# Search rounds spread over all tensor work, a new selection, sliding attention turned by DMA, and a gate projection moved

## The chip, the core and the metric

The kernel runs on one core of a Trainium2 chip. The metric is device time in microseconds for one execution. The profile follows five engines of the core: PE (TensorE, with its weight loads as PEld), DVE (VectorE), ACT (ScalarE), POOL (GpSimd) and SP (SyncE, which here only issues DMAs). Each takes its instructions in the order in which they were written for it.

## The reference

Two layers act on a sequence of 1024 tokens with 1024 channels. Each is an RMS norm, one input projection, two attentions whose outputs are multiplied by a gate `silu(z)`, and an output projection with a residual.

```
# layer 1
y = rms_norm(x) @ ab_w_in                    # qa ka va qi ki wi za qb kb vb zb
score = sum_h wi_h * relu(qi_h . ki)         # causal, per query
idx = top_k(score, 256)
oa = softmax(qa . ka over idx) @ va          # sparse attention, 8 heads, 2 key heads
ob = softmax with sinks over a window of 128 # sliding attention, 8 heads
x = x + concat(oa*silu(za), ob*silu(zb)) @ ab_w_out
# layer 2
oc = g0*compressed + g1*selected + g2*window attention
q  = rms_norm(cq,  d_q_lat_norm)  @ d_w_uq   # latent attention
kv = rms_norm(ckv, d_kv_lat_norm) @ d_w_ukv
od = causal softmax attention
x = x + concat(oc*silu(zc), od*silu(zd)) @ cd_w_out
```

The top-k of a query tile with 384 to 1024 causal keys (tiles 2 to 7; tiles 0 and 1 keep all keys) is needed exactly, ties resolved to the lower key index.

## The kernel before, in words

Everything is tiled by 128 tokens (8 tiles). A projection is cut into chunks of about 256 columns. For each chunk and each token tile, `fill_gen` issues 24 matmuls: the operands are split into a high and a low part, and three products (L498, L499, L500) are summed over 8 row blocks. The weights come by DMA from SP into `wraw` (L450), ACT makes the high part `whi` (L454), POOL the low part `wlo` (L455). The list `FAO` sets the order of the chunks of layer 1: `ki qi kb qb0 z0 z1 z2 qb1 ka qa0 qa1`. The `z` chunks are gates.

`attn_gen` walks a list of attention jobs. A job is one query tile and one key head, so four heads. The passes of q.k (L644, PE) go into `psS`; a DVE instruction (L647) adds the mask and leaves the scores and the negative row maximum `nm`; ACT takes the exponential with `nm` as bias (L652) into `pt`. Then up to four blocks of 128x128 at a time go through `tstage` and `cstage`: PE turns the blocks of `pt` (L672) into PSUM, they are split into two halves of 16 bits, `ph` and `pl`, scaled by `PSCALE` = 4096, and PE multiplies them with the values (L690, L691, L692). `WAYS` says how the split is made. Way `p`: ACT writes `ph` (L676) and DVE `pl` (L677). Way `q`: ACT copies to `sg` (L681), POOL writes `ph` (L682) and `pl` (L683). The sliding attention (`job_b`, 16 jobs) uses way `q` alone.

The top-k is a search for a threshold, bit by bit, on 32-bit keys that are kept as two 16-bit halves, `hi16` and `lo16`. `topk` runs 16 rounds on one half and 16 on the other. A round counts, for each tile, the keys under a candidate: tiles 2, 3 and 7 on DVE (L855), 4, 5 and 6 on ACT (L851), then two small DVE instructions move the candidate (L866, L868). After the 32nd round the selection turns the threshold into an additive mask, tile by tile: five passes over the keys on DVE (L900, L901, L903, L904, L906), one running sum (L905), and two POOL passes (L907, L908). A sparse attention job (`job_a`) of tile 2 or more waits for the mask of its tile.

`Lanes.run` interleaves the generators when the program is written: a main one (attention jobs), a filling one (projections, `ratio`), and the search (`aux`, `arate`). Each step of a generator gives its cost in nanoseconds of tensor work; a search round counts as 2000. In `run` at most one step of the search is taken for each step of the others, as long as its sum is under `TA` = 1.2 times their sum. When a job has to wait for a projection, `pump` issues projections until it is there; there the search gets no step. What is left of the search is issued after the last sliding job, by `while not searched`. Then a scheduler of the framework reorders the instructions of each engine. So the order has to be read from the built program.

Layer 2 has the same structure. Its latents `cq` and `ckv` are normed in `lat_chain` with a broadcast row of gains `glat` (L1353).

## Time and profile before

| | |
|---|---|
| three runs | 1542.68, 1544.64, 1548.07 us; median 1544.64 |
| profiled execution | 1548.08 us; its span 1546.3 us |
| mean granted clock of TensorE | 0.949 of full |
| PE busy | 1375.8 us (89%) |
| DVE busy | 1140.0 us (74%) |
| ACT busy | 898.8 us (58%) |
| POOL busy | 883.4 us (57%) |
| DMA | 93.18 MB, mean 60 GB/s |

The profile belongs to one execution, whose own time is 1548.08 us, 3.4 us above the median of the three. Busy time is the union of an engine's instructions; the rest of the span it waited. The share over the whole span mixes stretches that are bound by different engines, so the rows further below are cut by stretch.

### The profile page before, as it was taken

To read this page: it belongs to the slowest core of one execution; us is meant where nothing else is said; L and a number is where in the kernel's file an instruction comes from. 1 tells how busy PE (TensorE), PEld (TensorE's weight loads), DVE (VectorE), ACT (ScalarE), POOL (GpSimd) and SP (SyncE) were. 2 spreads that over 40 slices of the span, in tenths; PEclk is the share of its full clock that TensorE was granted. 3 is DMA by queue.
4 is the path that set the end of the run, shared out by engine and by line. 5 is a ranking of instruction groups with operands and counts; after the bars stand their busy time and mean duration, and the time that the engine had idled before them with its cause. 6 is when DMAs were issued, how large, how long until landed. Compare 5 with 4: busy or idle time off the path is not lost.

```text
span 1546.3 us, 35007 instructions
## 1 busy us (share of the span) xinstructions
PE 1375.8 (89%) x12588; PEld 1269.9 (82%) x12588; DVE 1140.0 (74%) x3431; ACT 898.8 (58%) x2451; POOL 883.4 (57%) x1194
## 2 busy tenths in 40 slices
PE   5998899865568989999999999999998678789998
PEld 5997799765467778999999998899987557678887
DVE  5387898889967856157257678976699989987763
ACT  5355698686337855145435567857666676655541
POOL 6798664885989576226255443575456566642240
PEclk9999999887779999999999999999999879989999
DMA  6311223010112233132211210011101120111232
GB/s 203 88 30 34 59 80 88 20 49 6 52 38 69 74 108 123 49 139 77 62 29 49 60 42 8 26 53 49 36 5 46 59 65 8 31 53 63 93 114 75
DMA packets 88431, 93.18 MB, mean 60 GB/s; under 512 B 20930, under 2 KB 73154, under 8 KB 88258
## 3 DMA queue, kind: packets, MB, share of 16 engines
q1 hardware_dynamic: 88256, 90.95, 19.7%
q8 instruction: 99, 1.62, 0.4%
q14 instruction: 76, 0.61, 0.1%
HBM read 67.85 MB, written 23.07 MB: 59 GB/s over the span
## 4 chain that ended last, share of the span: by engine, by line
PE 55%; DVE 23%; ACT 7%; issue 5%; DMA 5%; POOL 4%; SPq 1%; DVEq 0%; ACTq 0%; POOLq 0%
PE pp L498 8%; PE pp L500 8%; PE psS L644 8%; PE pp L499 8%; PE psT L672 6%; DVE pt L647 4%; ACT junka L851 3%; DMA wraw<-in_ab_w_in 2%; PE pp L1695 2%; PE pp L1697 2%; PE pp L1696 2%; PE po L692 2%; PE po L690 2%; PE po L691 2%; DVE pl L677 1%
## 5 line engine op out<-in xcount | busy, mean ns | idle before, releaser
L498 PE MATMUL pp<-whi,Rh 128*128 128x256 f32 (+4 forms) x1648 | 484.9, 295 | 27.9 <-ACT sq L432 10.8
L499 PE MATMUL pp<-wlo,Rh 128*128 128x256 f32 (+4 forms) x1648 | 477.0, 290 | 1.1 <-POOL wlo L455 1.1
L500 PE MATMUL pp<-whi,Rl 128*128 128x256 f32 (+4 forms) x1648 | 477.4, 290 | 0.0
L498 PEld LDWEIGHTS pp<-whi,Rh 128*128 128x128 f32 x1648 | 318.0, 193 | 34.2 <-ACT sq L432 12.3
L652 ACT ACTIVATE pt<-pt,nm 128x256 f32<-128x256 f32 (+8 forms) x384 | 246.3, 642 | 162.6 <-DVE nm L647 158.6
L499 PEld LDWEIGHTS pp<-wlo,Rh 128*128 128x128 f32 x1648 | 317.8, 193 | 3.1 <-POOL wlo L455 1.6
L500 PEld LDWEIGHTS pp<-whi,Rl 128*128 128x128 f32 x1648 | 317.4, 193 | 1.2
L455 POOL TENSOR_TENSOR wlo<-wraw,whi 128x256 fp32r<-128x256 f32 (+4 forms) x208 | 166.1, 805 | 140.4 <-ACT whi L454 129.4
L672 PE MATMUL psT<-identf,pt 128*128 128x128 f32 x1256 | 219.0, 288 | 13.0 <-DVE pl L677 5.1
L682 POOL TENSOR_SCALAR ph<-sg 128x512 f16<-128x512 f32 (+3 forms) x157 | 90.2, 577 | 141.7 <-ACT sg L681 124.2
L683 POOL TENSOR_TENSOR pl<-sg,ph 128x512 f16<-128x512 f32 (+3 forms) x157 | 165.9, 1060 | 8.3
L672 PEld LDWEIGHTS psT<-identf,pt 128*128 128x128 f32 x1256 | 150.1, 146 | 24.8 <-ACT pt L652 3.8
L454 ACT ACTIVATE whi<-wraw 128x256 fp32r<-128x256 f32 (+4 forms) x208 | 83.8, 415 | 119.6 <-DMA wraw<-in_ab_w_in 38.1
L677 DVE SCALAR_TENSOR_TENSOR pl<-psT,ph 128x512 f16<-128x512 f32 (+3 forms) x233 | 128.0, 558 | 23.9 <-ACT ph L676 23.2
L676 ACT ACTIVATE ph<-psT 128x512 f16<-128x512 f32 (+3 forms) x233 | 111.6, 492 | 51.9 <-PE psT L672 46.1
L690 PEld LDWEIGHTS <-ph 128*128 128x128 f16 x1256 | 116.8, 100 | 22.1 <-issue 7.1
L692 PEld LDWEIGHTS <-pl 128*128 128x128 f16 x1256 | 114.9, 100 | 20.9 <-POOL pl L683 6.8
L647 DVE CUSTOM_DVE_ANT_0 pt<-psS,mk 128x512 f32<-128x512 f32 (+4 forms) x208 | 107.7, 520 | 32.6 <-PE psS L644 29.7
L691 PEld LDWEIGHTS <-ph 128*128 128x128 f16 x1256 | 116.8, 100 | 12.0 <-issue 10.7
L681 ACT ACTIVATE sg<-psT 128x512 f32<-128x512 f32 (+3 forms) x157 | 83.1, 535 | 41.1 <-PE psT L672 34.0
L652 ACT ACTIVATION_READ_ACCUMULATOR pt<-pt,nm 128x1 f32 x384 | 73.1, 190 | 0.0
L1054 POOL TENSOR_TENSOR mo<-mo,nz 128x256 f32<-128x256 f32 (+1 forms) x32 | 32.2, 1009 | 68.9 <-DMA nz<-zdr 29.5
(311 smaller groups left out, 3583.4 us busy)
## 6 DMA issues: line engine op xcount, KB each, us to landing
wraw<-in_cd_w_in SPq DMA_DIRECT2D x72, 128.0 KB, 2.1
wraw<-in_ab_w_in SPq DMA_DIRECT2D x56, 128.0 KB, 2.1
xs<-in_x SPq DMA_DIRECT2D x8, 512.0 KB, 6.1
od<-mx SPq DMA_DIRECT2D x32, 128.0 KB, 1.8
wraw<-in_ab_w_out SPq DMA_DIRECT2D x32, 128.0 KB, 2.2
x<-in_x SPq DMA_DIRECT2D x8, 512.0 KB, 5.2
mo<-od SPq DMA_DIRECT2D x16, 256.0 KB, 2.7
nz<-zdr SPq DMA_DIRECT2D x16, 256.0 KB, 3.1
```

Source lines behind the costliest of these rows:

```text
L455: G.tensor_tensor(lo[:, :o], raw[:, :o], hi[:, :o].bitcast(F32), OP.subtract)
L498: T.matmul(ps, xh, hi[:, :n], start=q == 0 and k == 0, stop=False)
L499: T.matmul(ps, xh, lo[:, :n], start=False, stop=False)
L500: T.matmul(ps, xl, hi[:, :n], start=False, stop=q == 3 and k == 1)
L647: V.tensor_tensor_reduce(pt[:, j * nk + c:j * nk + c + w], ps[:, at:at + w], mask(c, w), -1.0, first, op0=OP.add, op1=OP.min, accum_out=low)
L652: S.activation(pt[:, j * nk:(j + 1) * nk], pt[:, j * nk:(j + 1) * nk], AF.Exp, scale=-1.0, bias=nm[:, h:h + 1], accum_out=sm[:, h:h + 1])
L672: T.transpose(pT[:, a], pt[:, o:o + P], identf)
L677: V.scalar_tensor_tensor(pl[:, :n], pT[:, :n], PSCALE, ph[:, :n], op0=OP.mult, op1=OP.subtract)
L683: G.tensor_tensor(pl[:, :n], sg[:, :n], ph[:, :n], OP.subtract)
L690: T.matmul(dst, ph[:, a], vh(kt, h), start=kt == 0, stop=False)
L691: T.matmul(dst, ph[:, a], vl(kt, h), start=False, stop=False)
L692: T.matmul(dst, pl[:, a], vh(kt, h), start=False, stop=kt == nt - 1)
```

## The change

It has six parts. (1) `Lanes.beside` takes steps of the search after every step of tensor work, in `pump` too, and as many as are due; the rate `TA` is 0.5 in place of 1.2. (2) After the 32nd round one more round of counts is made, which gives the number of ties to drop, and the selection then takes two ACT passes, four DVE instructions and one POOL pass for each tile. (3) The factor 4096 moves from the split into the exponential: ACT adds ln 4096 to `nm` once for each group of heads. (4) The sliding attention takes way `g`: right after the exponential ACT writes the high half of `pt` and POOL the low half side by side into `hl`, and a DMA from SP turns all of it into `ht`, so PE turns no block. The other ways write their halves into `ht` as well, and `sg` shares the buffers of `hl` (4 in place of 2). (5) The chunk `z2` stands behind `qa0`. (6) The gains of the latent norms are multiplied into the rows of `d_w_uq` and `d_w_ukv` in `small_w`, and the last stage's `xr` shares the buffers of `wraw2`.

```diff
-TA = 1.2
+TA = 0.5
-FAO = 'ki qi kb qb0 z0 z1 z2 qb1 ka qa0 qa1'
+FAO = 'ki qi kb qb0 z0 z1 qb1 ka qa0 z2 qa1'
-WAYS = ('q', 'q', 'ppq', 'pq', 'ppq', 'pq', 'ppq', 'p')
+WAYS = ('g', 'g', 'ppq', 'pq', 'ppq', 'pq', 'ppq', 'p')
...
+    def beside(self, c):
+        self.due += self.rate * (c or 0.0)
+        while self.aux is not None and self.spent < self.due:
+            try:
+                self.spent += next(self.aux)
+            except StopIteration:
+                self.aux = None
...
     def pump(self, fill, until=None):
...
             self.tick()
+            self.beside(c)
...
     def run(self, main, fill, ratio, aux=None, arate=0.0):
...
             m += y
             self.tick()
+            self.beside(y)
             while fill_on and f < ratio * m:
...
                 f += c
                 self.tick()
-                if aux_on and a < arate * (m + f):
-                    try:
-                        a += next(aux)
...
+                self.beside(c)
...
+                S.activation(nm[:, h0:h0 + per], nm[:, h0:h0 + per], AF.Copy, bias=LNP)
                 for j, h in enumerate(hs):
                     S.activation(pt[:, j * nk:(j + 1) * nk], pt[:, j * nk:(j + 1) * nk], AF.Exp, scale=-1.0,
...
+                    if way[-1] in "dg":
+                        o, w = c * P, n * P
+                        hl = wk.tile([P, 1024], F16, name="hl", bufs=HLB)[:, :2 * w]
+                        S.activation(hl[:, :w], pt[:, o:o + w], AF.Copy)
+                        (V if way[-1] == "d" else G).tensor_tensor(hl[:, w:], pt[:, o:o + w], hl[:, :w], OP.subtract)
+                        ht = wk.tile([P, 8, P], F16, name="ht", bufs=HTB)
+                        nc.sync.dma_start(ht[:, :2 * n], hl.rearrange("p (k n) -> p k n", n=P), transpose=True)
...
+        counts(lo16)
+        V.tensor_tensor(inc, cnt, tgt, OP.subtract)
+        for i in GA:
+            V.tensor_scalar(inc[:, i - 2:i - 1], inc[:, i - 2:i - 1], 0.5, None, op0=OP.mult)
+        yield 2000
         searched.append(1)
...
-            V.tensor_scalar(j, blk(hi16, i), K1[:, c], None, op0=OP.is_gt)
-            V.scalar_tensor_tensor(gt, blk(lo16, i), K0[:, c], j, op0=OP.is_gt, op1=OP.add, accum_out=cnt[:, c])
-            V.tensor_scalar(inc[:, c], cnt[:, c], -1.0, float(TOPK), op0=OP.mult, op1=OP.add)
-            V.tensor_scalar(j, blk(lo16, i), K0[:, c], None, op0=OP.is_equal)
-            V.scalar_tensor_tensor(eq, blk(hi16, i), K1[:, c], j, op0=OP.is_equal, op1=OP.mult)
+            S.activation(v, blk(hi16, i), AF.Identity, scale=-1.0, bias=K1[:, c])
+            S.activation(below, blk(lo16, i), AF.Identity, scale=-1.0, bias=K0[:, c])
+            V.scalar_tensor_tensor(v, v, 2.0 ** 18, below, op0=OP.mult, op1=OP.add)
+            V.tensor_scalar(eq, v, 0.0, None, op0=OP.is_equal)
             V.tensor_tensor_scan(pre, eq, eq, 0.0, op0=OP.add, op1=OP.max)
-            V.scalar_tensor_tensor(eq, pre, inc[:, c], eq, op0=OP.is_le, op1=OP.mult)
-            G.tensor_tensor(gt, gt, eq, OP.add)
-            G.tensor_scalar(blk(hi16, i).bitcast(BF16), gt, BIG, -BIG, op0=OP.mult, op1=OP.add)
+            V.scalar_tensor_tensor(v, pre, inc[:, c], v, op0=OP.is_gt, op1=OP.add)
+            G.tensor_scalar(blk(hi16, i).bitcast(BF16), v, 0.0, -BIG, op0=OP.is_gt, op1=OP.mult)
...
-        V.scalar_tensor_tensor(z, z, r[0], g, op0=OP.mult, op1=OP.mult)
+        V.tensor_scalar(z, z, r[0], None, op0=OP.mult)
...
+            S.activation(raw, raw, AF.Copy, scale=B["glat"][:, g + r:g + r + 1])
```

Three places of the built order show what is moved. The first is DVE at the selection. Before, the selection of the tile of 896 keys (L900 to L906, with `sel` and `junk`) stands between passes of the sliding attention (L647 with `mB`) and its small sums:

```order
L900 TENSOR_SCALAR junk_1452<-hi16_789,K1_1454 128x896
L726 TENSOR_SCALAR sm_4728<-sm_4728 128x4
L901 SCALAR_TENSOR_TENSOR sel_4766,cnt_1457<-lo16_791,K0_1455,junk_1452 128x896
L647 ISA pt_4836,nm_4834<-psS_4837,mB_98,sinkn_99 128x256
L647 ISA nm_4834 128x1
L728 RECIPROCAL rs_4813<-sm_4728 128x4
L647 ISA pt_4836,nm_4834<-psS_4844,mB_98,sinkn_99 128x256
```

Now the selections follow each other on DVE with nothing between them until the tile of 896 keys, right behind the added counts (L874) and the number of ties (L914, L916); only there the first pass of the sparse attention (tile 0) stands:

```order
L874 TENSOR_SCALAR junk,cnt<-lo_791,cand 128x1024
L914 TENSOR_TENSOR inc<-cnt,tgt 128x6
L916 TENSOR_SCALAR inc<-inc 128x1 x3
L929 SCALAR_TENSOR_TENSOR sel<-sel,junk 128x384
L930 TENSOR_SCALAR sel<-sel 128x384
L931 SCALAR_TENSOR_TENSOR junk<-sel 128x384
L932 SCALAR_TENSOR_TENSOR sel<-junk,inc,sel 128x384
L929 SCALAR_TENSOR_TENSOR sel<-sel,junk 128x512
L930 TENSOR_SCALAR sel<-sel 128x512
L931 SCALAR_TENSOR_TENSOR junk<-sel 128x512
L932 SCALAR_TENSOR_TENSOR sel<-junk,inc,sel 128x512
```

All sliding jobs stand ahead of round 18 now. From round 28 on, and through the selections up to the tile of 768 keys, PE has no instruction at all. Before, 20 of the 64 passes of the sliding attention stood behind round 32, and projections with them.

The second place is SP, in the second half of the sliding attention. Before, it issues weight loads (`wraw`), and stores of results (`od<-mx`):

```order
L450 DMA wraw_5195<-in_ab_w_in 128x256
L450 DMA wraw_5258<-in_ab_w_in 128x256
L755 DMA od_101<-mx_4313 128x256
L450 DMA wraw_5264<-in_ab_w_in 128x256
L450 DMA wraw_5382<-in_ab_w_in 128x256
L755 DMA od_101<-mx_4441 128x256
L450 DMA wraw_5388<-in_ab_w_in 128x256
```

Now the transposing DMAs, which wait for POOL's `hl`, stand in the same queue ahead of weight loads:

```order
L680 DMA_TRANSPOSE ht_2574<-hl_2571 128x8x128
L680 DMA_TRANSPOSE ht_2579<-hl_2576 128x8x128
L455 DMA wraw_3585<-in_ab_w_in 128x256
L455 DMA wraw_3591<-in_ab_w_in 128x256
L680 DMA_TRANSPOSE ht_2670<-hl_2667 128x8x128
L680 DMA_TRANSPOSE ht_2675<-hl_2672 128x8x128
L774 DMA od_101<-mx_2773 128x256
L455 DMA wraw_3918<-in_ab_w_in 128x256
```

There are 30 of them in the program. Counted over all engines in the order of the build, 4 to 39 matmuls, 21 in the median, stand on PE between the issue of one and the first matmul that reads it (L709, which was L690).

The third place is ACT, in a sliding job of the first half. Before, the exponentials (L652) follow DVE's maximum directly, and the evacuation `sg` follows PE's turning:

```order
L652 ACTIVATE pt,sm<-pt,nm 128x256 x2
L723 ACTIVATE es<-es 128x4
L851 ACTIVATE junka,cnt<-hi_789,cand 128x640
L588 ACTIVATE zst<-pp 128x274
L851 ACTIVATE junka,cnt<-hi_789,cand 128x768
L652 ACTIVATE pt,sm<-pt,nm 128x256
L681 ACTIVATE sg<-psT 128x512 x2
```

Now the addition of ln 4096 (L656) stands ahead of the exponentials (L658) and the copy to `hl` (L677) behind them; the search's counts (L870) lie between:

```order
L656 ACTIVATE nm<-nm 128x4
L870 ACTIVATE junka,cnt<-hi_789,cand 128x640
L658 ACTIVATE pt,sm<-pt,nm 128x256 x4
L870 ACTIVATE junka,cnt<-hi_789,cand 128x768
L677 ACTIVATE hl<-pt 128x512
L742 ACTIVATE es<-es 128x4
```

## Rows read from the trace of the kernel before

**Rows 1.** The page: busy us of each engine, share of the span, instructions.

```profile
PE 1375.8 (89%) x12588; PEld 1269.9 (82%) x12588; DVE 1140.0 (74%) x3431; ACT 898.8 (58%) x2451; POOL 883.4 (57%) x1194
```

**Rows 2.** Stretches: start:end, length, busy PE, PEld, DVE, ACT, POOL; clock, DMA, GB/s.

```profile
178.00:284.00 106.00, 98.68 (x882) 95.86 (x880) 92.60 (x270) 90.13 (x240) 58.45 (x81) 0.98 0.24 68
284.00:368.00 84.00, 56.50 (x485) 54.28 (x483) 69.67 (x183) 68.91 (x179) 66.00 (x106) 0.86 0.14 34
368.00:460.00 92.00, 57.12 (x414) 51.88 (x415) 78.24 (x159) 35.70 (x112) 76.00 (x70) 0.72 0.11 37
460.00:605.00 145.00, 131.90 (x1510) 115.99 (x1508) 107.97 (x310) 102.51 (x240) 107.18 (x135) 0.98 0.27 78
605.00:820.00 215.00, 212.50 (x1779) 209.77 (x1780) 107.12 (x317) 80.36 (x219) 85.01 (x124) 0.98 0.26 79
820.00:1150.00 330.00, 324.81 (x3494) 307.93 (x3494) 248.49 (x948) 213.37 (x639) 166.94 (x228) 0.99 0.13 38
1150.00:1375.00 225.00, 178.95 (x1659) 152.62 (x1658) 211.67 (x742) 150.03 (x428) 137.51 (x186) 0.88 0.14 43
```

**Rows 3.** Chain that ended last, 178 to 460 us: shares of that stretch.

```profile
by line: ACT junka L851 15.1%; issue 12.1%; DVE junk L855 5.6%; DVE pt L647 5.1%; PE pp L498 4.5%; PE pp L499 4.0%; PE pp L500 3.9%; DMA wraw<-in_ab_w_in 3.6%; DVE sel L901 3.1%; DVE junk L905 2.9%; PE psS L644 2.6%; DVE sel L904 2.4%; DVE 
```

**Rows 4.** DVE by line, 366 to 440 us: busy us, mean ns, idle before.

```profile
L905 DVE TENSOR_TENSOR_SCAN junk<-sel 128x384 f16<-128x384 bf16 (+5 forms) x6 | 11.1, 1844 | 0.0
...
L901 DVE SCALAR_TENSOR_TENSOR sel<-lo,K,junk 128x384 bf16<-128x384 uint16 (+5 forms) x6 | 9.0, 1498 | 0.0
...
L906 DVE SCALAR_TENSOR_TENSOR sel<-junk,inc,sel 128x384 bf16<-128x384 f16 (+5 forms) x6 | 7.4, 1237 | 0.0
...
L904 DVE SCALAR_TENSOR_TENSOR sel<-hi,K,junk 128x384 bf16<-128x384 int16 (+5 forms) x6 | 7.1, 1184 | 0.1
...
L900 DVE TENSOR_SCALAR junk<-hi,K 128x384 bf16<-128x384 int16 (+5 forms) x6 | 6.9, 1143 | 0.1
...
L903 DVE TENSOR_SCALAR junk<-lo,K 128x384 bf16<-128x384 uint16 (+5 forms) x6 | 3.3, 549 | 0.0
...
L726 DVE TENSOR_SCALAR sm<-sm 128x4 f32<-128x4 f32 x5 | 4.0, 807 | 0.0
```

**Rows 5.** POOL by line, 366 to 440 us: the rows beside the selection.

```profile
L683 POOL TENSOR_TENSOR pl<-sg,ph 128x512 f16<-128x512 f32 x10 | 14.1, 1428 | 0.0
...
L907 POOL TENSOR_TENSOR sel<-sel 128x384 bf16<-128x384 bf16 (+5 forms) x6 | 9.8, 1641 | 14.1 <-DVE sm L725 12.1 <-DVE sel L906 1.9
```

**Rows 6.** DVE by form, 178 to 284 us: the counts of a search round.

```profile
L855 DVE TENSOR_SCALAR_CACHE_REDUCE junk<-hi,cand 128x1024 bf16<-128x1024 int16 x16 | 20.4, 1276 | 0.3
...
L855 DVE TENSOR_SCALAR_CACHE_REDUCE junk<-hi,cand 128x512 bf16<-128x512 int16 x16 | 11.9, 741 | 0.2
...
L855 DVE TENSOR_SCALAR_CACHE_REDUCE junk<-hi,cand 128x384 bf16<-128x384 int16 x16 | 9.8, 610 | 0.4
```

**Rows 7.** ACT by form, whole run: the copy to `sg`, a copy of 128x4.

```profile
L681 ACT ACTIVATE sg<-psT 128x512 f32<-128x512 f32 x121 | 70.8, 592 | 37.1 <-PE psT L672 30.3 <-POOL pl L683 4.3 <-PE psS L644 0.8
...
L723 ACT ACTIVATE es<-es 128x4 f32<-128x4 f32 x16 | 3.1, 196 | 2.8 <-DVE es L721 2.8
```

**Rows 8.** POOL by form, whole run: the two passes of way `q`.

```profile
L683 POOL TENSOR_TENSOR pl<-sg,ph 128x512 f16<-128x512 f32 x121 | 144.7, 1199 | 5.9
L682 POOL TENSOR_SCALAR ph<-sg 128x512 f16<-128x512 f32 x121 | 77.0, 639 | 109.1 <-ACT sg L681 95.7 <-PE psS L644 9.2 <-PE psT L672 1.5
```

**Rows 9.** PE busy in the turning (L672) from 178 to 460 us.

```profile
sum 282.00, PE 25.98 PEld 16.83; mean PE 8.66 PEld 5.61
```

**Rows 10.** Waits of the whole run: us in total, times, longest us.

```profile
ACT pt L652 <- DVE nm L647: 158.6, 146, 5.1
```

**Rows 11.** DMA issues: count, KB each, median us to landing.

```profile
xr<-x1d SPq DMA_DIRECT2D x16, 256.0 KB, 3.1
```

**Rows 12.** DMA `pe` of 128x16 short runs: us from issue to landing.

```profile
DMA to landing us min/median/max: 3.2/5.5/7.9
```

More of the change, by code (lines that the diff above doesn't have):

```diff
@@ L39 @@
 PSCALE = 4096.0
+LNP = float(np.log(PSCALE))
+HLB = 4
+HTB = 4
 SLOT = 2048
@@ L46 @@
 WB = 2
-XB = 2
 WP = 2
@@ L84, in __init__ @@
         self.live = {}
+        self.aux, self.rate, self.due, self.spent = None, 0.0, 0.0, 0.0
     def post(self, gen):
@@ L128, in run @@
     def run(self, main, fill, ratio, aux=None, arate=0.0):
-        m = f = a = 0.0
+        m = f = 0.0
         fill_on = fill is not None
-        aux_on = aux is not None
+        self.aux, self.rate, self.due, self.spent = aux, arate, 0.0, 0.0
         for y in main:
@@ L149, in run @@
                 self.tick()
[L150 to L159 removed]
+                self.beside(c)
+        self.aux = None
 @with_exitstack
@@ L662, in attn_gen @@
                     todo = [(2 * a, 0, a * P) for a in range(2)]
+                way, turned = [], []
+                for c in range(0, len(todo), 4):
+                    n = min(4, len(todo) - c)
+                    way.append(next(jb["way"]))
+                    ht = None
+                    if way[-1] in "dg":
[5 more added lines that the diff above has]
+                        nc.sync.dma_start(ht[:, :2 * n], hl.rearrange("p (k n) -> p k n", n=P), transpose=True)
+                    turned.append(ht)
                 for c in range(0, len(todo), 4):
@@ new lines, in tstage @@
+                        if way in "pq":
+                            ht = wk.tile([P, 8, P], F16, name="ht", bufs=HTB)
+                            pT = tps()
+                            for a, (h, kt, o) in enumerate(grp):
+                                T.transpose(pT[:, a], pt[:, o:o + P], identf)
+                        ph, pl = ht[:, :n], ht[:, n:2 * n]
+                        if way == "p":
+                            S.activation(ph, pT[:, :n], AF.Copy)
+                            V.tensor_tensor(pl, pT[:, :n], ph, OP.subtract)
+                        elif way == "q":
+                            sg = wk.tile([P, 4, P], F32, name="sg", tag="hl", bufs=HLB)
+                            S.activation(sg[:, :n], pT[:, :n], AF.Copy)
+                            G.tensor_scalar(ph, sg[:, :n], 1.0, 1.0, op0=OP.mult, op1=OP.mult)
+                            G.tensor_tensor(pl, sg[:, :n], ph, OP.subtract)
@@ L696, in cstage @@
                             return n * 87 + (0 if not lastg else 1)
-                        return cstage, n * 110
+                        return cstage, n * 110 if way in "pq" else 1
                     tq.append(tstage)
@@ L1342, in lat_pre, with lat_chain @@
         D["kx"] = ks_[:, 1024:2048].rearrange("p (a b n) -> p a b n", a=2, b=2)
-        B["glat"] = cc.tile([P, 384], F32, name="glat")
-        nc.sync.dma_start(B["glat"][:, 0:256], row(A["d_q_lat_norm"][0], 0, 256))
-        nc.sync.dma_start(B["glat"][:, 256:384], row(A["d_kv_lat_norm"][0], 0, 128))
+        B["glat"] = cc.tile([P, 3], F32, name="glat")
+        nc.sync.dma_start(B["glat"][:, 0:2], A["d_q_lat_norm"][0].rearrange("(k p) -> p k", p=P))
+        nc.sync.dma_start(B["glat"][:, 2:3], A["d_kv_lat_norm"][0].rearrange("(k p) -> p k", p=P))
         G.tensor_scalar(B["glat"], B["glat"], RG, 1.0, op0=OP.mult, op1=OP.mult)
-    def lat_chain(z, ss, n, g, dst):
+    def lat_chain(z, ss, n, dst):
         yield
@@ L1362, in lat_chain, with lat_start @@
         L.give("psT")
-    def lat_start(ps, n, g, dst):
+    def lat_start(ps, n, dst):
         L.take("nz", NZ)
@@ L1459, in wout_gen, with small_w @@
                     yield
-    def small_w(ap, rows, n, tag):
+    def small_w(ap, rows, n, tag, g):
         hi = D["pool"].tile([P, rows, n], F32R, name="wh" + tag)
@@ L1557, in next_query @@
         if (i, g) == (0, 0):
-            D["wuq", 1] = small_w(wq[:, 384:768], 2, 384, "q")
+            D["wuq", 1] = small_w(wq[:, 384:768], 2, 384, "q", 0)
     def d_prologue():
@@ L1689, in out_tile @@
         for c in range(2):
-            xr = D["pool"].tile([P, 512], F32, name="xr", bufs=XB)
+            xr = D["pool"].tile([P, 512], F32, name="xr", tag="wraw2", bufs=WB)
             cs_ = slice(512 * c, 512 * c + 512)
@@ L1747, in trunk @@
             L.tick()
-    D["wkv", 1] = small_w(wkv[:, 512:1024], 1, 512, "kv")
+    D["wkv", 1] = small_w(wkv[:, 512:1024], 1, 512, "kv", 2)
     FD = d_fill()
```

45 lines of the change are left out of this document (11 added, 34 removed).

## Prediction

> **What bounds the kernel now.** I first read the busy times of the whole span [rows 1]: PE is busy for 89% of it, so a microsecond taken from another engine counts only in a stretch where PE waits. Those stretches show in the windows [rows 2], cut at the first search round (178 us), the 17th (284), the 32nd (368), the first pass of the sparse attention with a mask (460) and the end of layer 1's sparse attention (605). From 605 to 820 us PE is busy for 212.5 of 215 us: what is saved elsewhere there is worth nothing. From 1150 to 1375 us DVE is (211.7 of 225). From 178 to 460 us nobody is full: DVE 92.6 + 69.7 + 78.2 = 240.5 of 282 us, PE 98.7 + 56.5 + 57.1 = 212.3, and PE's clock falls to 0.86 and 0.72. So I read the chain there [rows 3]: counts of the search on ACT (15.1%) and DVE (5.6%), the selection on DVE, little of PE. DVE, and the hand-overs of the search between DVE and ACT, set the time up to 460 us. Last I read DVE and POOL between 366 and 440 us, where the selection lies [rows 4, 5].
>
> **Part 2, the selection.** The five passes and the running sum cost DVE 6.9 + 9.0 + 3.3 + 7.1 + 11.1 + 7.4 = 44.8 us [rows 4]. The new one keeps four of their kind: the product-and-sum (like L904, 7.1), the comparison (L903, 3.3), the running sum (11.1) and the last pass (7.4), together 28.9. So 6.9 + 9.0 = 15.9 us go. One more round of counts comes, 1.28 + 0.74 + 0.61 = 2.6 us [rows 6], and four small instructions, an estimated 0.5. Net -12.8 us. What replaces L900 and L901 are two ACT passes per tile, and ACT is busy for 35.7 of 92 us there [rows 2]; as they don't depend on one another, ACT runs ahead of DVE.
>
> The selection lay beside POOL's full load (76 of 92 us). POOL's subtraction L683 took 1428 ns there [rows 5] against 1199 over the run [rows 8], 19% more, and the small sum L726 of 4 columns 807 ns [rows 4]. Both engines stretch when both work. The built order shows the new selections without PE and POOL work between them, so the 28.9 us could shrink by the same 16% (1 - 1199/1428), 4.6 us. Ends: -12.8 (no relief) and -17.4 (all of it). I take -17, since the order shows POOL with one pass per tile there in place of L907 (9.8 us) and L908. The Trainium skill, page "VectorE: DVE Perf Modes", has DVE and POOL share a port; these rows agree in direction, and no sum above needs it.
>
> **Part 1, even issue.** It moves counts and removes none. The whole sliding attention now stands ahead of round 18, and PE is empty from round 28 to the tile of 768 keys: an estimated 5 rounds of 2.6 + 0.6 us and 24 us of selections, some 40 us less what I count for overlap, 33 us. Does PE's work fit into the rest? After the turning is gone (26.0 us [rows 9]) it is 212.3 - 26.0 = 186 us, in 282 - 17 - 33 = 232 us: 80%, where 178 to 284 us shows 98.7/106 = 93%. It fits. What could be won is DVE's idle time, 282 - 240.5 = 41.5 us. The search needs ACT and DVE in turn in every round, with sliding passes before and after, so I expect that most of it remains. Ends: 0 and -20 (half). I take 0: this is the end nearest to the row of 178 to 284 us, where counts and sliding work were already mixed well and DVE still had 13 us idle of 106. The later start of the 32nd round (an estimated 421 us) is no loss in itself, since what stood behind it is done before.
>
> **Part 4, the turning.** It takes 26.0 us from PE [rows 9] and 30 x 0.64 = 19 us (L682) from POOL; ACT copies 128x512 as before (592 ns [rows 7]) and POOL subtracts as before. All of it lies under DVE's load, so it is worth 0, as long as the transfers are in time. The trace has no transposing DMA. The nearest by size are plain DMAs of 256 KB, 3.1 us from issue to landing [rows 11]; the nearest by the shape of many short runs are those of `pe`, median 5.5 us, up to 7.9 [rows 12]. The cover is the 21 matmuls in the median that stand between issue and use: 212.5 us/1779 = 0.119 us each where PE is full [rows 2], 2.5 us, or an estimated 3 us with PE's waits. At 3.1 us nothing is late; at 5.5 us each use waits 2.5 us, 30 x 2.5 = 75 us, of which PE's slack of 232 - 186 = 46 takes up the larger part: +29. I take 0, by the row nearest in size, and keep +29 as the other end. If a transfer is late, its P.V products are late, then the buffers `ht` and `hl`, then ACT. On SP a transposing DMA waits for POOL's `hl` with weight loads queued behind it; the loads run ahead by two buffers and SP is issued early, so I count nothing.
>
> Against this edit stands a rule of the Trainium skill, page "VectorE: DVE Perf Modes", section "The three transpose paths": a block of 128x128 goes through TensorE in 390 ns and through the DMA crossbar in 1309 ns, so TensorE is to be used if PSUM will do as a destination. By it 8 blocks, taken one after the other, make an estimated 10.5 us. The page "Advanced Engine Details and Errata", section "X-Bar Transpose (TRN2)", says the opposite, that transposing DMAs are as fast as regular ones. No run here shows either yet; by the second page the sum stays as it is.
>
> **Part 3, ln 4096 on ACT.** There is one such copy of 4 columns for each group of heads, 208 in the program, at 196 ns [rows 7]: 41 us of ACT over the run. Where PE is full they are hidden by PE. Where DVE and ACT alternate they lengthen the way from maximum to exponential, on which ACT waits 146 times, 158.6 us in all [rows 10]. I count 44 groups of the masked attention (460 to 605 us, PE 91%) and about 30 of the stretch from 1150 to 1375 us, 74 x 0.2 = 15 us at most, 20 with the hand-over to itself; the other end is 0, as jobs overlap. The row of 460 to 605 us is nearer to full PE than to waiting, so I take +6.
>
> **Parts 5 and 6.** They lie where PE is full (605 to 820 us) or in the first 178 us; the two rows of small_w's extra ACT pass are hidden by PE. 0. Without that cover it would be some 10 passes of 0.4 to 0.6 us (as L681), 5 us.
>
> **Sum.** 1548.1 - 17 + 0 + 0 + 6 = 1537 for the profiled execution. That one lies 3.4 us above the median of the three runs, so the forecast is 1537 - 3.4 = 1534 us (1533.7).
>
> **Rivals.** 0.3%, about what a measurement of this kernel tells from no change, is 4.6 us: 1540.0 to 1549.3 counts as the same.
> - A, the forecast: 1534, its own range 1524 to 1544 (from -17 - 10 with part of DVE's idle time closed and no cost of ln 4096, to the cost of +16). 0.46.
> - B, the even issue closes half of DVE's idle time (up to -20) as PE's projections fill what was waiting: 1534 - 14 to -20 = 1514 to 1520. For it speaks the clock of 0.72 to 0.86; against it that a round needs both engines in turn. 0.14.
> - C, no net gain: -12.8 and a price of ln 4096 and its hand-overs of 10 to 17 us: 1541 to 1549. For it speaks the 158.6 us of waits [rows 10]. 0.12.
> - D, the other side: transfers land late. The price is 30 x (L - 3) - 46 for a landing time L in us; it passes the forecast's gain of 11 us from L = (11 + 46)/30 + 3 = 4.9 us on. At 5.5 us [rows 12] it is +29, 1563; the place is the sliding attention, PE waiting in L709. 0.24.
> - E, the blocks of a transfer run one after the other at a rate below the demand: the stage then lasts as long as the transfers. From the rows alone I bound it with the worst `pe`, 7.9 us [rows 12]: 30 x 4.9 - 46 = +101, 1635. By the page that speaks for TensorE it would be an estimated 30 x 7.5 - 46 = +180 us. 0.04: no row shows a plain transfer of this size near that.
>
> **How the numbers follow.** The time is that of A. Faster: 0.43 of A's 0.46 (some of it reaches past 1540) and B's 0.14: 0.57. Same: 0.02 of A and C's 0.12: 0.14. Slower: D, E and the tip of A, 0.29. The range runs from below B, 1508, to past D's middle, 1568; outside lie E, the late part of D and a larger B, together 0.2.
>
> **What would show it.** In the profile after: selection passes on DVE (six tiles) of 24 to 29 us in all, no L900 or L901 of before; the first masked pass of the sparse attention at an estimated 441 to 449 us in place of 460; transposing DMAs landing within 3 to 4 us, and P.V of the sliding attention waiting for them under 10 us in all; ACT's wait for `nm` not above 165 us; the stretch of the masked attention 145 to 150 us long; everything behind it as long as before to within 5 us. The 32nd round near 421 us with PE empty for some 33 us behind round 28 is the even issue as read from the order. I am wrong if the landing times are above 5 us and L709 waits for them, if the span up to the first masked pass doesn't shrink, or if DVE's idle time between 178 and 460 us falls by more than 10 us (then B).

## The result, and the profile after

| | median us | range | runs |
|---|---|---|---|
| before | 1548.07 | 1542.68 to 1549.25 | 5 |
| changed | 1535.34 | 1535.19 to 1540.21 | 5 |

The ratio is 0.9945, 95% interval 0.9928 to 0.9962: 0.55% faster, clear of the 0.3%. (It is the measure used below; the plain quotient of the two medians in the table is 0.9918.) The forecast was 1534. The profiled execution took 1535.34 us, its span 1533.5. The time is close, but that was luck: the experiments below show that the sum reached it with three wrong terms that cancel in part.

The page of the changed kernel; it answers to [rows 1]:

```profile
PE 1354.2 (88%) x12468; PEld 1244.5 (81%) x12468; DVE 1129.9 (74%) x3417; ACT 940.7 (61%) x2683; POOL 850.2 (55%) x1158
```

PE lost 120 instructions (the turned blocks) and 21.6 us, ACT gained 41.9 us and POOL lost 33.2 us.

The windows of the changed kernel, with the columns of [rows 2], cut at the same events of the program: the end of the sliding attention's P.V and of the first half of the search (335), the 32nd round (406.3), the first masked pass (442.7), the last (584.6), the first pass of layer 2's selected attention (801.2), the first pass of the latent attention (1237.8):

```profile
178.00:335.00 157.00, 138.19 (x1293) 131.69 (x1292) 136.83 (x392) 131.90 (x401) 118.47 (x156) 0.94 0.50 105
335.00:406.30 71.30, 47.18 (x362) 45.96 (x361) 61.46 (x147) 59.08 (x134) 48.04 (x72) 0.86 0.17 51
406.30:442.70 36.40, 6.86 (x24) 4.54 (x25) 30.50 (x56) 13.93 (x26) 13.07 (x6) 0.50 0.08 29
442.70:584.60 141.90, 128.89 (x1481) 112.81 (x1479) 105.89 (x308) 111.13 (x289) 96.17 (x120) 0.98 0.26 76
584.60:801.20 216.60, 213.20 (x1792) 210.13 (x1790) 108.83 (x321) 82.08 (x222) 86.82 (x126) 0.98 0.27 80
801.20:1237.80 436.60, 402.42 (x4248) 372.11 (x4247) 344.07 (x1328) 293.96 (x954) 221.71 (x315) 0.97 0.13 38
1237.80:1533.50 295.70, 266.89 (x2184) 225.16 (x2184) 223.48 (x659) 162.02 (x433) 123.11 (x156) 0.96 0.20 66
```

And the kernel before, cut at the same events (460.1, 603.6, 820.9, 1248.3):

```profile
178.00:460.10 282.10, 212.40 (x1778) 202.12 (x1777) 240.51 (x611) 194.74 (x528) 200.55 (x256) 0.86 0.17 48
460.10:603.60 143.50, 131.30 (x1505) 115.53 (x1505) 106.57 (x307) 101.15 (x237) 105.68 (x134) 0.98 0.26 77
603.60:820.90 217.30, 213.90 (x1795) 211.04 (x1792) 109.42 (x323) 82.11 (x222) 87.05 (x126) 0.98 0.27 80
820.90:1248.30 427.40, 399.42 (x4248) 372.25 (x4247) 340.64 (x1326) 278.64 (x844) 223.84 (x314) 0.96 0.14 40
1248.30:1546.30 298.00, 269.64 (x2186) 228.07 (x2184) 226.69 (x661) 155.15 (x389) 123.40 (x157) 0.95 0.20 64
```

Each stretch belongs to one execution of each kernel. Up to the first masked pass 17.4 us are gained (282.1 to 264.7), DVE's busy time fell by 11.7 us (240.5 to 136.8 + 61.5 + 30.5 = 228.8). The masked attention gains 1.6 us. From 584.6 to 801.2 nothing moves (216.6, before 217.3). Then 9.2 us are lost in the stretch where PE is busiest with layer 2's attentions (427.4 to 436.6), although PE's busy time grows by 3 us only: it waits more. The rest gains 2.3 us (298.0 to 295.7). The sum is -12.8 us, the difference of the spans.

The first and last start of the masked passes (`hi`) and of the sliding ones (`sinkn`), with shortest, median and longest ns, in the changed kernel:

```profile
L652 DVE CUSTOM_DVE_ANT_0 pt<-psS,hi x48: 480/689/692, 442.7 to 583.2; 128x512 f32<-128x512 f32 x32, 128x384 f32<-128x384 f32 x8, 128x320 f32<-128x320 f32 x8
...
L652 DVE CUSTOM_DVE_ANT_0 pt<-psS,mB,sinkn x56: 446/479/485, 171.0 to 308.5; 128x256 f32<-128x256 f32 x56
```

442.7 lies within the 441 to 449 that I gave. The selection on DVE by line (busy us, mean ns, idle before), which answers to [rows 4]:

```profile
L931 DVE TENSOR_TENSOR_SCAN junk<-sel 128x384 f16<-128x384 bf16 (+5 forms) x6 | 9.8, 1625 | 0.2
L932 DVE SCALAR_TENSOR_TENSOR sel<-junk,inc,sel 128x384 bf16<-128x384 f16 (+5 forms) x6 | 5.7, 950 | 0.1
L929 DVE SCALAR_TENSOR_TENSOR sel<-sel,junk 128x384 bf16<-128x384 bf16 (+5 forms) x6 | 5.4, 892 | 4.0 <-ACT junk L928 3.9
L930 DVE TENSOR_SCALAR sel<-sel 128x384 bf16<-128x384 bf16 (+5 forms) x6 | 3.5, 583 | 0.2
```

Together 24.4 us: 28.9 less the 16% that I had estimated is 24.3. The new waits are small: DVE waits 3.9 us for ACT's second pass L928, which writes the one `junk` that the tile before still reads.

The transposing DMAs, their issue on SP, and who waited for them (us, times):

```profile
L680 SPq DMA_TRANSPOSE ht<-hl x30: 1231/1239/2202, 182.8 to 321.6; - x30
...
  PEld L709: 2.8, 5
...
  PE po L709: 1.8, 4
...
DMA to landing us min/median/max: 3.0/3.2/5.1
```

They land in 3.2 us in the median and 5.1 at most, and PE waits for them at most 4.6 us in all (2.8 + 1.8; matmuls and weight loads can wait at the same time). The Trainium skill, page "VectorE: DVE Perf Modes", section "The three transpose paths", gives 1309 ns for a block, which I made an estimated 10.5 us for 8. This trace does not bear the estimate out: 8 blocks land 3.2 us after their issue in the median. The trace agrees with the page "Advanced Engine Details and Errata", section "X-Bar Transpose (TRN2)", that such DMAs are as fast as regular ones: the plain ones of 256 KB `xr<-x1d` take 3.1 us in the kernel before [rows 11].

### The profile page after: what moved, and what is told of

Read it like the earlier page. It is cut to its first block, busy times and chain, and to the rows that moved or that the text cites. A ratio compares the mean times of both kernels' runs of the same rounds, so it can differ in the third digit from the quotient of the medians.

```text
span 1533.5 us, 34714 instructions
## 1 busy us (share of the span) xinstructions
PE 1354.2 (88%) x12468; PEld 1244.5 (81%) x12468; DVE 1129.9 (74%) x3417; ACT 940.7 (61%) x2683; POOL 850.2 (55%) x1158
## 5 line engine op out<-in xcount | busy, mean ns | idle before, releaser
L658 ACT ACTIVATE pt<-pt,nm 128x256 f32<-128x256 f32 (+8 forms) x384 | 244.3, 639 | 3.5
L693 PE MATMUL psT<-identf,pt 128*128 128x128 f32 x1136 | 195.7, 284 | 13.9 <-ACT pt L658 5.4
L459 ACT ACTIVATE whi<-wraw 128x256 fp32r<-128x256 f32 (+4 forms) x208 | 83.8, 415 | 133.0 <-DMA wraw<-in_cd_w_in 41.9
L693 PEld LDWEIGHTS psT<-identf,pt 128*128 128x128 f32 x1136 | 133.8, 144 | 29.5 <-ACT pt L658 11.7
L701 POOL TENSOR_SCALAR ht<-sg 128x512 f16<-128x512 f32 (+3 forms) x127 | 69.5, 548 | 136.0 <-ACT sg L700 99.5
L696 ACT ACTIVATE ht<-psT 128x512 f16<-128x512 f32 (+3 forms) x233 | 112.4, 493 | 52.9 <-PE psT L693 46.0
L697 DVE TENSOR_TENSOR ht<-psT,ht 128x512 f16<-128x512 f32 (+3 forms) x233 | 128.3, 558 | 14.8 <-ACT ht L696 14.3
L711 PEld LDWEIGHTS <-ht 128*128 128x128 f16 x1256 | 114.8, 100 | 26.9 <-DVE ht L697 10.6
L709 PEld LDWEIGHTS <-ht 128*128 128x128 f16 x1256 | 116.5, 100 | 20.5 <-issue 5.1
L702 POOL TENSOR_TENSOR ht<-sg,ht 128x512 f16<-128x512 f32 (+3 forms) x127 | 127.3, 1003 | 7.4
L652 DVE CUSTOM_DVE_ANT_0 pt<-psS,mk 128x512 f32<-128x512 f32 (+4 forms) x208 | 107.9, 521 | 31.6 <-PE psS L649 25.5
L710 PEld LDWEIGHTS <-ht 128*128 128x128 f16 x1256 | 116.6, 100 | 6.5 <-issue 5.3
L649 PE MATMUL psS<-ka,qs 128*128 128x512 f32 (+4 forms) x192 | 56.9, 393 | 51.5 <-DVE nm L652 51.5
L656 ACT ACTIVATE nm<-nm 128x1 f32<-128x1 f32 (+2 forms) x208 | 41.8, 202 | 97.5 <-DVE nm L652 96.7
L700 ACT ACTIVATE sg<-psT 128x512 f32<-128x512 f32 (+3 forms) x127 | 66.6, 525 | 26.4 <-PE psT L693 25.5
```

Of the source, the lines that this page charges most:

```text
L658: S.activation(pt[:, j * nk:(j + 1) * nk], pt[:, j * nk:(j + 1) * nk], AF.Exp, scale=-1.0, bias=nm[:, h:h + 1], accum_out=sm[:, h:h + 1])
L693: T.transpose(pT[:, a], pt[:, o:o + P], identf)
L696: S.activation(ph, pT[:, :n], AF.Copy)
L697: V.tensor_tensor(pl, pT[:, :n], ph, OP.subtract)
L702: G.tensor_tensor(pl, sg[:, :n], ph, OP.subtract)
L709: T.matmul(dst, ph[:, a], vh(kt, h), start=kt == 0, stop=False)
```

## The experiments

Each kernel is the changed one or the one before with one edit. The table gives the ratio to the kernel before on the same chip, and from each kernel's profile the first masked pass, the stretch from there to the first pass of layer 2's selected attention, from there to the first latent pass, and the rest to the end.

| kernel | median us | ratio, interval | masked | to selected | to latent | rest |
|---|---|---|---|---|---|---|
| before | | 1 | 460.1 | 360.8 | 427.4 | 298.0 |
| changed | 1535.34 | 0.9945, 0.9928 to 0.9962 | 442.7 | 358.5 | 436.6 | 295.7 |
| e1 selection only | 1531.65 | 0.9920, 0.9900 to 0.9939 | 449.3 | 361.5 | 425.5 | 295.0 |
| e2 old selection | 1547.86 | 1.0016, 0.9999 to 1.0033 | 451.3 | 361.6 | 435.6 | 296.3 |
| e3 no turning by DMA | 1533.50 | 0.9933, 0.9913 to 0.9953 | 437.8 | 360.6 | 437.2 | 296.1 |
| e4 old rule of issue | 1537.38 | 0.9957, 0.9940 to 0.9974 | 445.4 | 356.1 | 434.9 | 297.0 |
| e5 no ln 4096 | 1521.72 | 0.9851, 0.9823 to 0.9879 | 443.8 | 352.1 | 428.8 | 294.8 |
| e6 z2 at its old place | 1542.11 | 0.9985, 0.9967 to 1.0004 | 445.8 | 363.5 | 437.5 | 297.5 |
| e7 selection, gains | 1525.59 | 0.9878, 0.9851 to 0.9906 | 450.5 | 359.2 | 426.9 | 291.1 |
| e8 selection, even issue, z2 | 1515.32 | 0.9805, 0.9775 to 0.9834 | 432.3 | 356.2 | 423.1 | 297.9 |
| e9 copy behind | 1523.64 | 0.9854, 0.9836 to 0.9872 | 449.1 | 354.5 | 426.1 | 294.1 |
| e10 head by head | 1530.59 | 0.9902, 0.9882 to 0.9923 | 440.8 | 357.6 | 432.8 | 300.7 |
| e11 selection, even issue | 1529.22 | 0.9894, 0.9874 to 0.9914 | 448.3 | 356.1 | 426.4 | 296.7 |
| e12 turning counted | 1535.43 | 0.9939, 0.9921 to 0.9956 | 447.3 | 356.1 | 438.2 | 291.4 |

The four columns on the right come from one execution of each kernel. In their time, e1, e3, e4, e9 and e10 came out as my first expectation had them. e2, e5, e7 and e8 were faster than expected, e6 slower, and e11 and e12 took the time of the rival that stands beside the expectation.

**The selection: e1 and e2.** In e1 the kernel before gets the new one, in e2 the changed kernel gets the old one:

```diff
+        counts(lo16)
+        V.tensor_tensor(inc, cnt, tgt, OP.subtract)
...
-            V.tensor_scalar(j, blk(hi16, i), K1[:, c], None, op0=OP.is_gt)
-            V.scalar_tensor_tensor(gt, blk(lo16, i), K0[:, c], j, op0=OP.is_gt, op1=OP.add, accum_out=cnt[:, c])
...
+            S.activation(v, blk(hi16, i), AF.Identity, scale=-1.0, bias=K1[:, c])
+            S.activation(below, blk(lo16, i), AF.Identity, scale=-1.0, bias=K0[:, c])
```

> The kernel before with the new selection alone (the added counts, two ACT passes, four DVE instructions, one POOL pass); everything else as before. My theory: the selection is the whole gain before the first masked pass, so about 1531 to 1535 us where the kernel before has 1548 (-13 to -17), first masked pass at 443 to 447 us in place of 460. The rival that the gain comes from the even issue or the turning: 1542 to 1548.

> The changed kernel with the old selection put back (five passes and a running sum on DVE, no added counts). My theory: the gain before the masked attention goes, 1548 to 1553 us (+13 to +17 on the changed kernel), first masked pass at 456 to 460. The rival that the even issue or the turning made the gain: 1535 to 1540.

Alone it is worth 0.8% (e1), within the changed kernel 0.7% (1.0016 to 0.9945): 11 to 12 us of the kernel before's 1545, less than my 17. The first masked pass came at 449.3 us in e1, where I expected 443 to 447, and at 451.3 in e2, where I expected 456 to 460. So e2 shows what the selection alone can't explain: the other parts gain 8.8 us before the masked attention (460.1 to 451.3), and lose it again in layer 2 (427.4 to 435.6). In e1, without them, layer 2 takes 425.5 us: the loss belongs to the other parts (to 3, 4 or 6, as e8 below has 423.1).

**The turning by DMA: e3 and e12.** e3 lets PE turn the sliding attention, e12 keeps the DMAs and changes the account from which the search gets its steps:

```diff
-WAYS = ('g', 'g', 'ppq', 'pq', 'ppq', 'pq', 'ppq', 'p')
+WAYS = ('q', 'q', 'ppq', 'pq', 'ppq', 'pq', 'ppq', 'p')
```

> The changed kernel with the sliding attention turned by TensorE again (way q), no transposing DMA. My theory: TensorE has room there, so within 3 us of the changed kernel's 1535. The rival that the turning made room for the even issue (26 us of TensorE work come back in a stretch where all of it must fit ahead of round 28): 1545 or more, the 32nd round later than 415 us.

```diff
-                        return cstage, n * 110 if way in "pq" else 1
+                        return cstage, n * 110
```

> The changed kernel where a step of the sliding attention turned by DMA is still counted as 110 ns for each block in the account that decides when the search gets its next step (the changed kernel counts 1). Turned by TensorE the first masked pass came at 437.8 us, by DMA at 442.7. Theory: the turning itself costs nothing, the account holds the search back by 13 us of tensor work, some 3 rounds: first masked pass at 437 to 440, the 32nd round before 400 (406 in the changed kernel), run at 1530 to 1534. Rival: the transfers or SP's issue of 1.24 us each hold the work up: first masked pass at 442 to 445 and 1535.

The turning by DMA changes the time by nothing that can be measured (0.9933 without, 0.9945 with: 2 us, known to some 4). In the profile of e3 the first masked pass stood 4.9 us earlier; I thought that the account was the cause, and e12 refutes it: 447.3, no earlier than with the account of 1. e5 and e9 below differ by copies that turn out to cost nothing, and stand 5.3 us apart there (443.8 and 449.1), so 4.9 us in one execution prove little.

**ln 4096: e5, e9 and e10.** e5 leaves the copy (and with it the factor 4096) out. e9 has the copies behind the exponentials, without the addition (the factor is left out there as well):

```diff
-                S.activation(nm[:, h0:h0 + per], nm[:, h0:h0 + per], AF.Copy, bias=LNP)
                 for j, h in enumerate(hs):
                     S.activation(pt[:, j * nk:(j + 1) * nk], pt[:, j * nk:(j + 1) * nk], AF.Exp, scale=-1.0,
                                  bias=nm[:, h:h + 1], accum_out=sm[:, h:h + 1])
+                S.activation(nm[:, h0:h0 + per], nm[:, h0:h0 + per], AF.Copy)
```

e10 adds it head by head:

```diff
-                S.activation(nm[:, h0:h0 + per], nm[:, h0:h0 + per], AF.Copy, bias=LNP)
                 for j, h in enumerate(hs):
+                    S.activation(nm[:, h:h + 1], nm[:, h:h + 1], AF.Copy, bias=LNP)
                     S.activation(pt[:, j * nk:(j + 1) * nk], pt[:, j * nk:(j + 1) * nk], AF.Exp, scale=-1.0,
```

> The changed kernel without ln 4096: the copies of 4 columns on ACT are gone and the exponentials are not scaled (this leaves the factor out of the computation, all else stays). The stretch from layer 2's first compressed or selected attention pass to its first latent attention pass lasted 427 us before, 425 us with the selection alone and 437 us in the changed kernel. Theory: the copies between DVE's maximum and the exponential are what makes it longer, so it comes back to 425 to 429 and the run to 1525 to 1529 us. Rival: the folded gains (part 6) or the shared buffers do it: the stretch stays at 434 to 438 and the run at 1533 to 1537.

> The changed kernel with the copy of 4 columns put behind the exponentials, without the addition (the factor 4096 is left out): ACT has the same 208 copies, but no exponential stands behind one. Theory: the price of ln 4096 is the way from maximum to exponential, so 1521 to 1525 us as without the copies (1521.7). Rival: it is ACT's time, 208 x 0.2 us: 1533 to 1537 as in the changed kernel.

> The changed kernel with ln 4096 added head by head, right before each exponential: 384 copies in place of 208, and the first exponential of a group no longer waits for the maxima of all its heads. If the wait for the whole group was the price: 1526 to 1531 us. If ACT's time or the length of each copy on the way is the price: 176 copies more, 1536 to 1546.

Without the copies the run is 0.95% shorter (0.9945 to 0.9851), 14 us. In the two profiles 6.4 us of it lie between the first masked pass and layer 2's selected attention (358.5 to 352.1) and 7.8 in the stretch after (436.6 to 428.8). The second place is sure: all six kernels with one copy for a group ahead of the exponentials take 434.9 to 438.2 us for that stretch, the seven without a copy there 423.1 to 428.8, whatever their other parts. The first is not: there the two kinds overlap (356.1 to 363.5 and 352.1 to 361.5). e9 settles how the copies cost time: the same number of copies on ACT, behind the exponentials, costs nothing that can be measured (0.9854). So it is not ACT's time but the place on the way from DVE's maximum to the exponential. The copies and their durations in the changed kernel by form:

```profile
L656 ACT ACTIVATE nm<-nm 128x1 f32<-128x1 f32 x128 | 25.8, 202 | 54.0 <-DVE nm L652 53.4
...
L656 ACT ACTIVATE nm<-nm 128x4 f32<-128x4 f32 x48 | 9.7, 202 | 36.9 <-DVE nm L652 36.9
...
L656 ACT ACTIVATE nm<-nm 128x2 f32<-128x2 f32 x32 | 6.4, 200 | 6.6 <-DVE nm L652 6.4
```

Who waited behind it: the waits of the changed kernel over the whole run (total us, times, longest):

```profile
ACT nm L656 <- DVE nm L652: 96.7, 86, 6.0
...
PEld psS L649 <- DVE nm L652: 87.8, 68, 45.7
...
DVE sm L745 <- ACT pt L658: 23.8, 30, 3.0
```

and those of e5:

```profile
ACT pt L657 <- DVE nm L652: 127.9, 128, 4.4
...
DVE sm L744 <- ACT pt L657: 9.5, 21, 1.0
```

The longest wait of PE for a maximum, 45.7 us, is the time in which the search ends and the selections run. DVE's small sum of the softmax waits 23.8 us for the exponentials, 9.5 without the copies, and in e9 it waits as little:

```profile
DVE sm L745 <- ACT pt L657: 11.7, 23, 1.4
```

e10 has 176 copies more and is still 0.4% shorter than the changed kernel (the intervals, 0.9882 to 0.9923 and 0.9928 to 0.9962, just don't meet): the wait of a group's first exponential for the maxima of all its heads is part of the price. About half remains. I put it down to the copy itself, as 128 of the 208 groups have one head; no run takes that part further apart.

**Even issue and z2: e4, e6, e8, e11.** e4 puts the old rule of issue back into the changed kernel, e6 the old order of chunks. e8 adds both to e1, e11 the even issue alone. The edit of e4:

```diff
-TA = 0.5
+TA = 1.2
...
-                self.beside(c)
+                if aux_on and a < arate * (m + f):
+                    try:
+                        a += next(aux)
```

and of e6:

```diff
-FAO = 'ki qi kb qb0 z0 z1 qb1 ka qa0 z2 qa1'
+FAO = 'ki qi kb qb0 z0 z1 z2 qb1 ka qa0 qa1'
```

> The changed kernel with the old rule of issue (at most one step of the search for a step of the others, none in pump, TA 1.2). My theory: the even issue is worth nothing by itself, within 3 us of 1535. The rival that it closed DVE's idle time: 1541 to 1550, with more DVE idle time between 178 us and the first masked pass than the 36 us of the changed kernel.

> The changed kernel with z2 back at its old place in the order of the chunks. My prediction: worth 0, so within 3 us of the changed kernel's 1535, first masked pass within 2 us of 442.7. Rival: the order of z2 lets the sparse attention of the first tiles run before the masks and made the part of the gain that the selection alone does not give (449 against 443 us): first masked pass at 447 or later.

> The kernel before with the new selection, the even issue and the new place of z2 (parts 2, 1, 5), and neither ln 4096, nor the turning by DMA, nor the folded gains. Theory: the first masked pass at 436 to 440 us as without the turning, layer 2 as before: 1518 to 1523 us, faster than both kernels. Rival: the loss in layer 2 belongs to the new order of issue: 1530 to 1534.

> The kernel before with the new selection and the even issue, z2 at its old place. Selection alone gave 1531.65 us, selection with even issue and the new place of z2 1515.3. Theory now: the place of z2 is worth about 7 us, as in the changed kernel, and the even issue the rest: 1520 to 1525, first masked pass near 436. Rival: the even issue only pays with z2 out of the way: 1529 to 1533.

e8 is the fastest kernel of the study: 0.9805, 1515.3 us. The even issue alone adds nothing sure to e1 (0.9920 to 0.9894), with z2's new place it is 1.2% (0.9920 to 0.9805). In the changed kernel the old rule of issue costs nothing sure (0.9957 against 0.9945), the old place of z2 0.4%. So it is z2's place that carries it: 0.9% over e11 (0.9894 to 0.9805). The selection with z2's new place but the old rule of issue was not run; that the rule adds nothing to it is read from e4. The q.k passes of the sliding attention (`kb`), first and last start, in e11 (even issue, old place), in e4 (old rule, new place) and in e8 (both new):

```profile
L648 PE MATMUL psS<-kb,qs x128: 220/281/583, 163.2 to 401.0; 128*128 128x256 f32 x112, 128*128 128x128 f32 x16
```

```profile
L655 PE MATMUL psS<-kb,qs x128: 220/281/581, 164.6 to 307.7; 128*128 128x256 f32 x112, 128*128 128x128 f32 x16
```

```profile
L648 PE MATMUL psS<-kb,qs x128: 222/282/579, 162.8 to 323.7; 128*128 128x256 f32 x112, 128*128 128x128 f32 x16
```

With z2 at its old place the last of them starts at 401.0 us, as before (412.3) and beside the selection; with z2 behind `qa0` at 307.7 even under the old rule. The second half of the sliding attention needs `qb1`, which stood behind z2. z2 fills time behind it instead: the eight copies of its results by ACT, 270 columns wide, start between 231.9 and 254.1 us in the kernel before and between 345.7 and 370.9 in the changed one. In e6, with z2 at its old place but the sliding attention turned by DMA, the last of those passes starts at 372.8 us, ahead of the selection, which goes with the smaller worth of z2's place there. In e8's windows PE's clock up to the first masked pass is 0.90, against 0.86 before, and 1.00 in the masked attention, which is 138.4 us long:

```profile
178.00:432.30 254.30, 206.08 (x1813) 196.11 (x1812) 225.83 (x594) 202.61 (x544) 203.36 (x263) 0.90 0.18 53
432.30:570.70 138.40, 125.45 (x1464) 108.90 (x1463) 104.65 (x303) 100.88 (x237) 96.09 (x120) 1.00 0.26 79
788.50:1211.60 423.10, 396.43 (x4248) 369.41 (x4247) 338.05 (x1326) 279.04 (x844) 224.55 (x314) 0.97 0.13 40
```

DVE is idle for 28.5 us ahead of it (254.3 - 225.8), for 41.6 in the kernel before and 35.9 in the changed one.

**The folded gains: e7.** e1 with part 6 (without the shared buffers of `xr`):

```diff
-        V.scalar_tensor_tensor(z, z, r[0], g, op0=OP.mult, op1=OP.mult)
+        V.tensor_scalar(z, z, r[0], None, op0=OP.mult)
...
+            S.activation(raw, raw, AF.Copy, scale=B["glat"][:, g + r:g + r + 1])
```

> The kernel before with the new selection and the folded gains (part 6 without the shared buffers of xr). Theory (ln 4096 is the cost in layer 2): the stretch from the first selected pass to the first latent pass stays at 424 to 428 us, the run at 1530 to 1533. Rival: the folded gains cost it, by ACT's extra passes ahead of the latent attention: 433 to 437 us, the run at 1538 to 1543.

They cost nothing: 0.9878 after 0.9920; the intervals overlap slightly (0.9900 to 0.9906), so a gain of 0.4% is likely rather than shown.

## Why the prediction came out near, point by point

The runs can be chained: selection alone 0.9920, with even issue and z2 0.9805, with the turning, the gains and the new storage but without ln 4096 0.9851, with all 0.9945. On 1545 us that is about -12, -18, +7 and +15 us (by the intervals the first to some 3 us, the others to some 6), together -8.5. My sum had -17, 0, 0 and +6, together -11.

- **Selection, taken as -17: the sum was mis-sized.** It is worth 11 to 12 us, near the lower end of -12.8, which held no relief. The new passes do take the 24.4 us that I had worked out with POOL's load gone. But the old passes are relieved as well where the other parts are in place. In e2 they take 37.8 us on DVE in place of 44.8 [rows 4]:

```profile
L920 DVE SCALAR_TENSOR_TENSOR sel<-lo,K,junk 128x384 bf16<-128x384 uint16 (+5 forms) x6 | 10.6, 1758 | 0.4
L924 DVE TENSOR_TENSOR_SCAN junk<-sel 128x384 f16<-128x384 bf16 (+5 forms) x6 | 9.7, 1623 | 0.2
L923 DVE SCALAR_TENSOR_TENSOR sel<-hi,K,junk 128x384 bf16<-128x384 int16 (+5 forms) x6 | 5.7, 952 | 0.2
L925 DVE SCALAR_TENSOR_TENSOR sel<-junk,inc,sel 128x384 bf16<-128x384 f16 (+5 forms) x6 | 5.7, 951 | 0.2
L922 DVE TENSOR_SCALAR junk<-lo,K 128x384 bf16<-128x384 uint16 (+5 forms) x6 | 3.7, 610 | 0.0
L919 DVE TENSOR_SCALAR junk<-hi,K 128x384 bf16<-128x384 int16 (+5 forms) x6 | 2.4, 403 | 0.2
```

So within the changed kernel the selection saves 37.8 - 24.4 = 13.4 us, less 2.6 of counts and 0.5 of small instructions: 10.3, and e2 shows 11. In e1, which has none of the other parts, DVE's busy time up to the first masked pass fell by 15.7 us (240.5 to 224.8), but DVE's idle time grew from 41.6 to 46.5 us, and the pass came only 10.8 us earlier. The window of e1, its chain that ended last in the 69 us ahead of that pass, and the same of the kernel before, in the 70 us ahead of it:

```profile
178.00:449.30 271.30, 212.01 (x1785) 201.03 (x1785) 224.80 (x590) 203.07 (x542) 197.06 (x251) 0.86 0.17 50
```

```profile
by line: POOL hi L914 17.7%; POOL pl L683 11.6%; POOL ph L682 10.6%; PE pp L498 6.6%; PE pp L499 5.9%; PE psS L644 5.7%; PE pp L500 5.6%; POOL rp_t L328 4.0%; DVE junk L855 3.0%; DVE junk L912 2.9%; PE psT L672 2.8%; DVE nz L364 2.4%; PE ps
```

```profile
by line: issue 9.3%; DVE junk L905 8.5%; DVE sel L901 7.6%; DVE sel L906 7.2%; PE pp L498 6.7%; DVE sel L904 6.7%; DVE junk L900 6.5%; DVE pt L647 6.0%; PE pp L499 5.3%; PE pp L500 5.2%; PE psS L644 4.4%; DVE ka L407 3.4%; ACT qs L374 3.4%;
```

Before, the selection on DVE leads that chain and POOL is not among the items named. With DVE relieved POOL leads it: its mask pass L914 stands between the splits of the sliding attention (L682, L683). My sum counted DVE's time alone.

- **Parts 1 and 5, taken as 0 each: wrong.** The step that failed is "Parts 5 and 6. They lie where PE is full (605 to 820 us) or in the first 178 us". z2 does not lie there: it stood ahead of `qb1`, between 178 and 260 us, and held the second half of the sliding attention back. From the built order I read that all sliding jobs stand ahead of round 18 now, and put it down to the even issue, to which I gave 0. What rival B expected, -14 to -20, is what e8 shows over e1, but by z2's place, not by the rule of issue.
- **Part 4, taken as 0: right, as far as e3 can tell.** The landing was 3.2 us in the median against the 3.1 of the row I chose. Rivals D and E are refuted by the landing times.
- **Part 3, taken as +6: the sum was mis-sized, and one reason was wrong.** The measured price is +14. I worked out 15 us at most from 74 groups of 0.2 us and then took less than half of it, because PE was near to full in the masked attention, and hid the rest under PE between 605 and 1150 us. In the stretch from 801 to 1238 us that cover held in part only. The same stretch of the changed kernel and of e5, each cut where ACT makes its last high part of a weight (`whi`), near the end of the projections:

```profile
801.20:1092.80 291.60, 283.62 (x3011) 267.79 (x3010) 210.42 (x783) 191.94 (x619) 139.25 (x190) 0.99 0.14 41
1092.80:1237.80 145.00, 118.80 (x1240) 104.32 (x1239) 133.65 (x546) 102.01 (x336) 82.46 (x125) 0.92 0.10 32
```

```profile
795.90:1084.70 288.80, 285.13 (x3050) 269.80 (x3049) 212.91 (x796) 188.12 (x566) 142.28 (x193) 1.00 0.14 41
1084.70:1224.70 140.00, 114.26 (x1201) 99.62 (x1200) 126.92 (x533) 92.87 (x286) 81.16 (x121) 0.92 0.10 33
```

While projections fill PE (busy for 283.6 of 291.6 us), 69 copies cost 2.8 us; behind them, where PE is busy for 118.8 of 145.0 us, 35 copies cost 5.0 (against e9 in place of e5 it is 2.3 and 8.2). There the attention's chain (q.k, maximum, exponential, turning) sets when PE's next work is ready. The first exponential of a group also waits for all of its heads, which I had not counted at all; and most copies are not of 4 columns, as I wrote, but of one (128 of 208), at the same 0.2 us. Rival C named the price (10 to 17 us) and a net of nothing; z2 kept it from coming true. The lower end of A's own range does not follow from its terms either: -17 and -10 without a price of ln 4096 make 1518, not 1524.
- **Part 6, taken as 0:** not a cost; possibly a gain (e7).

Of the other checks that I set, the selection (24.4 us), the first masked pass, the median landing time and the waits for it came out as stated; the masked attention was shorter (141.9 us in place of 145 to 150), the 32nd round earlier (406 in place of 421), PE empty for longer ahead of the masks (45.7 us in place of 33), and what lies behind them was not as long as before: the stretch to the latent attention is 9.2 us longer. My check on ACT's wait for `nm` ("not above 165 us") could not have shown the price: it fell from 158.6 us [rows 10] to 96.7, while what grew is what stands behind the copy.

Open: the +7 us between e8 and e5, not much above the noise, which the gains (e7) don't explain. In the profiles they arise ahead of the first masked pass: it starts at 432.3 us in e8 and at 443.8 in e5, and DVE is idle there for 28.5 and 42.6 us. The five kernels with the selection, the even issue, z2's new place and the turning by DMA have it at 440.8 to 449.1, the two that turn on PE instead at 432.3 (e8) and 437.8 (e3). That points at the turning, but e3's time is hardly shorter than the changed kernel's. The loss could also lie in the storage shared by `sg`, `hl`, `ht` and `xr`, or in the order that the framework's scheduler makes of it; this was not tried.
